# An output projection by seven products of half blocks in a transformer block kernel on one Trainium2 core

## The chip, the cores and the metric

The kernel runs on one core of a Trainium2 chip. The metric is device time in microseconds of one execution. Before the change three runs took 2075.6, 2077.8 and 2077.84 us; the median is 2077.8 us. The engines are named as the profile names them: PE (matrix products and transposes), PEld (its weight loads), DVE (vector engine), ACT (scalar engine), POOL and SP (the engine that issues nearly all DMAs here).

## The reference

One block on x of 512 positions by 2048 features, all in float32. What is computed:

```python
h = rmsnorm(x, g_attn)
proj = h @ w_in                                  # 2048 -> 6*1024 + 8
o_sb  = stick_breaking_attention(qa, ka, va)     # 8 heads of 128
o_fox = forgetting_attention(qf, kf, vf, log_f)  # 8 heads, softmax with a running bias
mixed = concat(head_rmsnorm(o_sb), head_rmsnorm(o_fox))    # 512 x 2048
x = x + mixed @ w_out                            # 2048 x 2048: the output projection
u = relu(rmsnorm(x, g_mlp) @ w_up)               # 2048 -> 8192
x = x + (u*u) @ w_down                           # 8192 -> 2048
return rmsnorm(x, g_final)
```

## The kernel before

Each float32 operand is split into a high part, a cast by ACT into a format that PE multiplies quickly (L63), and a low part, source minus high part by DVE (L64). A product is then three matmuls: high by high, high by low, low by high (`mm3`, L95 to L98). So each block of weights costs one DMA, one ACT cast, one DVE subtraction and its matmuls.

The stages on PE, in order: the projections of queries, keys and values, with the 16 attention heads laid between them (to about 627 us); the output projection (627 to 816 us); the up projection in 32 units (816 to 1400 us); the down projection (to 2010 us); the tail.

The output projection (`out_product`, L230) is plain. For each of four column blocks of 512 it loads 8 pieces of w_out (two rows of 128 by 512 columns), splits them and the matching two heads of `mixed`, and multiplies: 4 row blocks of 128 positions by 16 heads by 3 matmuls, into four banks `acco`. After a column block the residual is added (`x2`, L587), the sum is transposed back (`tr`, L597), and `a_form` makes the seven left sides that the up projection needs, split into `fh` and `fl`.

The up projection already multiplies by a scheme of seven products (Strassen and Winograd): a unit takes a 2 by 2 arrangement of blocks of w_up and needs sums of them. For 24 of the 32 units (`early`, L156) these sums are made during the projections: `drip` (L159) loads three blocks into the buffer `mix` (`sums`), does three DVE subtractions (L173 to L175) and stores the result in DRAM (`td`). The other 8 units load the blocks as they are ("raw" units) and do the three subtractions in the up stage (L677, L678, L680). `Unit.product` is one product: 8 matmuls of 512 columns with the high weights (against high and low left sides side by side) and 8 of 256 columns with the low ones.

The order of PE's instructions is written out for the projections and heads: `in_turn` yields after each piece with its nominal time, and parts of heads are put in when their step's time has come (`tc.manual_schedule`, L540). All else (DVE, ACT, SP, and PE in the later stages) is ordered by the compiler's scheduler; each engine executes its list in order, and each SP list entry is issued in order. A tile pool gives memory back when its `__exit__` runs; a tile that takes its place must wait for the last reader (`mixp_cm.__exit__`, L613, then `rw`, L620).

The forgetting heads need a bias row on all partitions: `bias_of` (L351) makes it by a matmul with a selector (`ck`) and an ACT copy (`cb`).

Of the kernel before, what the change touches and what calls it, by code (L numbers as in the profile page):

```python
# [14 lines left out]
P = 128  # L15
# [4 lines left out]
NH = 8  # L20
# [11 lines left out]


# [5 lines left out]
def block_kernel(ctx, tc, x, g_attn, w_in, b_f, g_out_sb, g_out_fox, w_out, g_mlp, w_up, w_down, g_final, y):  # L39
# [105 lines left out]
    md = [dp.tile([P, NT], F32, name=f"md{h}") for h in range(2 * NH)]  # L145
    td = [dp.tile([P, 3, KC // 2, P], F32, name=f"td{u}") for u in range(NU)]
    up_rows = w_up.rearrange("(a i p) f -> i p a f", i=2, p=P)

    def load_sums(u, i):

        r = mixp.tile([P, 3, KC // 2, P], F32, tag=f"x{i % 2}", name="sums")
        for j, (i, c) in enumerate(((0, 2 * u), (0, 2 * u + 1), (1, 2 * u + 1))):
            sp.dma_start(r[:, j], up_rows[i][:, :, c * P:(c + 1) * P])
        return r

    early = [u for u in range(NU) if u % 4 != 3]  # L156
    drops, raws, waiting = [0], {}, []

    def drip(low, load):  # L159

        drops[0] += 1
        i, j = divmod(drops[0] * 4 - 20, 9)
        with tc.issue_after(load.ins):
            if drops[0] == 2:
                raws.update((k, load_sums(early[k], k)) for k in range(2))
            if waiting and (waiting[0][0] <= drops[0] or (j < 4 and waiting[0][1] == i)):
                k = waiting.pop(0)[1]
                raws[k] = load_sums(early[k], k)
        if j > 3 or not 0 <= i < len(early):
            return  # L170
        b11, b12, b22 = (raws[i][:, j] for j in range(3))
# [4 lines left out]
        sp.dma_start(td[early[i]], raws.pop(i))  # L176
        if i + 2 < len(early):
            waiting.append((drops[0] + 2, i + 2))

    with (  # L180
        tc.tile_pool(name="hp", bufs=1) as hp,
        tc.tile_pool(name="att", bufs=1, side="right") as at,
    ):
# [14 lines left out]
        def accumulate_v(c0, m, steps, prepare=None, more=None):  # L198
# [7 lines left out]
            for j, step in enumerate(steps):  # L206
                k0, k1 = k1, k1 + step
                if prepare is not None:
                    prepare(k0, step)
                w = load_w([w_in[k0 * P:(k0 + step) * P, c:c + m // len(c0)].rearrange("(a p) c -> p a c", p=P) for c in c0],  # L210
                           step, m)
                held += [(k0 + i, w[i]) for i in range(step)]
# [17 lines left out]
        def out_product(n, mixed):  # L230
            ps = [acc.tile([P, NT], F32, tag="acc", name="acco") for _ in range(TB)]
            held = []
            for k0 in range(0, 2 * NH, 2):
                e0 = order[k0]
                w = load_w(w_out[e0 * P:(e0 + 2) * P, n * NT:(n + 1) * NT].rearrange("(a p) c -> p a c", p=P), 2, NT)
                ms = []
                for i in range(2):
                    ms.append(u_tile((k0 + i) % 4))
                    split(*ms[i], mixed[k0 // NH][:, (k0 + i) % NH, :])
                held += [(k0 + i, ms[i], w[i]) for i in range(2)]  # L240
                if n == 0 and k0 == 0:
                    continue
                for t in range(TB):
                    ts = slice(t * P, (t + 1) * P)
                    for k, m, wk in held:
                        mm3(ps[t], m[0][:, ts], m[1][:, ts], *wk, k == 0, k == 2 * NH - 1)
                    yield len(held) * 3 * 0.2267
                held = []
            return ps
# [101 lines left out]
        def bias_of(h):  # L351
            ck = atp.tile([P, NT], F32, tag="o", name="ck")
            pe.matmul(ck, nsel[:, h, :], ckT, start=True, stop=True)
            cb = at.tile([P, NT], F32, tag="ul5", name="cb")
            act.copy(cb, ck)
            return cb

        def attend_fox(h, hc, here):
# [3 lines left out]
            for i, r in enumerate(rows(s)):  # L362
                dve.scalar_tensor_tensor(rows(w)[i], r, cq[:, i, h:h + 1], cb[:, :(i + 1) * P], op0=ALU.add, op1=ALU.add)
# [15 lines left out]
        order = [NH + h for h in (6, 7, 0, 1, 2, 3, 4, 5)] + list(range(NH))  # L379
# [4 lines left out]
        with tc.tile_pool(name="tr0", bufs=2, space=PSUM) as trp:  # L384
# [56 lines left out]
            nsel = at.tile([P, NH, P], F32R, name="nsel")  # L441
            sel = wide("w")[:, :NH * P].rearrange("p (a b) -> p a b", a=NH)
            pool.memset(sel, 0.0)
            for shift in (0, NH):
                pool.affine_select(out=sel, in_=sel, compare_op=ALU.not_equal, fill=-1.0, base=-shift,
                                   pattern=[[-1, NH], [0, P]], channel_multiplier=1)
            dve.tensor_copy(nsel, sel)

        with tc.tile_pool(name="attp", bufs=1, space=PSUM) as atp:
# [3 lines left out]
            chl = at.tile([P, TB, P], F32, name="chl")  # L453
            pool.memset(chl, 0.0)
            cr = at.tile([P, TB, NH], F32R, name="cr")
# [18 lines left out]
            act.copy(cr, cq)  # L474
            dve.tensor_copy(chl[:, :, :NH], cr.bitcast(F32))
            dve.tensor_tensor(chl[:, :, NH:2 * NH], cq, cr.bitcast(F32), op=ALU.subtract)
            ckT = at.tile([P, NT], F32R, name="ckT")

            def turn_bias():
                cT = atp.tile([P, NT], F32, tag="o", name="cT")  # L480
                for t in range(TB):
                    pe.transpose(cT[:, t * P:(t + 1) * P], chl[:, t, :], ident)
                act.copy(ckT, cT)

            U, CB = {}, {}
            late = {}
# [15 lines left out]
            def outputs():  # L502
                late["mixed"] = [mixp.tile([P, NH, NT], F32, tag=f"x{i}", name="mixed") for i in range(2)]
                for k in range(2 * NH - 2):
# [495 lines left out]
```

## Time and profile before

| | us |
|---|---|
| median of three runs | 2077.8 |
| the profiled execution, its own time | 2075.16 |
| its span, first to last instruction | 2073.1 |
| PE busy in it | 2053.1 |
| DVE busy | 1601.9 |
| ACT busy | 1071.9 |
| clock granted to PE, mean | 0.999 of full |

The busy time of PE comes from modelled ends of pipelined matmuls; the distance between the starts of two matmuls is the better price of one. Idle time of an engine matters only where PE waits for it.

### The profile page before, as it was taken

What the parts mean: (1) busy time and instruction counts of PE and PEld (TensorE: products, weight loads), DVE (VectorE), ACT (ScalarE), POOL (GpSimd) and SP (SyncE); (2) the same over time, 40 slices, a digit from 0 to 9 for tenths busy, and PEclk for the clock granted to TensorE, in tenths of its full rate; (3) what the DMA queues carried; (4) which work ended last, traced back from release to release, by engine and by line L of the source; (5) the groups of instructions that cost most, each with busy time, mean ns of one, the idle gap of its engine ahead of it and who ended that gap; (6) DMA issues with size and microseconds to landing.
All of it is one profiled execution on the core that took longest, in us unless ns stands there. A gap on an engine that the chain in (4) does not pass through costs nothing.

```text
span 2073.1 us, 26761 instructions
## 1 busy us (share of the span) xinstructions
PE 2053.1 (99%) x10292; PEld 1746.6 (84%) x10292; DVE 1601.9 (77%) x1827; ACT 1071.9 (52%) x1426; POOL 57.1 (3%) x77
## 2 busy tenths in 40 slices
PE   9999999999999999999999999999999999999998
PEld 8888888888888887888888888888888888888886
DVE  5747748748766657788888888888799989888885
ACT  6334434444546556666666666666744434443433
POOL 0000000001100000000000000000000000000003
PEclk9999999999999999999999999999999999999999
DMA  7948948948833445578778777778865764764732
GB/s 237 296 134 255 295 150 259 315 116 254 289 102 102 132 152 171 178 260 273 237 257 272 243 252 265 234 253 285 321 232 209 266 240 163 266 232 135 271 111 82
DMA packets 356575, 455.88 MB, mean 220 GB/s; under 512 B 11440, under 2 KB 255200, under 8 KB 347360
## 3 DMA queue, kind: packets, MB, share of 16 engines
q1 hardware_dynamic: 355488, 452.05, 65.9%
q10 hardware_dynamic: 960, 2.13, 0.3%
q8 instruction: 81, 1.33, 0.2%
q14 instruction: 46, 0.38, 0.0%
HBM read 347.17 MB, written 106.95 MB: 219 GB/s over the span
## 4 chain that ended last, share of the span: by engine, by line
PE 90%; DVE 4%; DMA 3%; issue 2%; ACT 1%; SPq 0%; ACTq 0%; DVEq 0%
PE psa L687 9%; PE accd L96 8%; PE accd L98 8%; PE accd L97 8%; PE accq L96 5%; PE accq L98 5%; PE accq L97 5%; PE psa L689 5%; PE psc L687 4%; PE acco L97 3%; PE acco L98 3%; PE acco L96 3%; PE accv L96 3%; PE accv L97 3%; PE accv L98 3%; PE psc L689 2%
## 5 line engine op out<-in xcount | busy, mean ns | idle before, releaser
L63 ACT CAST wh<-wraw 128x1024 fp32r<-128x1024 f32 (+2 forms) x133 | 135.4, 1018 | 196.1 <-PE accq L97 115.5
L63 ACT CAST wh<-wd 128x1024 fp32r<-128x1024 f32 (+1 forms) x136 | 135.1, 1000 | 182.8 <-PE accd L98 120.6
L64 DVE TENSOR_TENSOR wl<-wraw,wh 128x1024 fp32r<-128x1024 f32 (+2 forms) x133 | 157.9, 1188 | 81.2 <-ACT wh L63 78.7
L64 DVE TENSOR_TENSOR wl<-wu,wh 128x1024 fp32r<-128x1024 f32 x166 | 201.8, 1223 | 17.7 <-PE psa L689 5.4
L63 ACT CAST wh<-wu 128x1024 fp32r<-128x1024 f32 x166 | 172.1, 1049 | 72.6 <-PE psa L687 25.1
L96 PE MATMUL accq<-hH,wh 128*128 128x512 f32 x512 | 201.2, 393 | 0.0
L98 PE MATMUL accq<-hH,wl 128*128 128x512 f32 x512 | 200.1, 391 | 0.0
L97 PE MATMUL accq<-hL,wh 128*128 128x512 f32 x512 | 199.8, 390 | 0.0
L64 DVE TENSOR_TENSOR wl<-wd,wh 128x1024 fp32r<-128x1024 f32 (+1 forms) x136 | 155.8, 1156 | 39.2 <-ACT wh L63 38.9
L96 PE MATMUL accd<-wh,uf 128*128 128x512 f32 x436 | 169.8, 389 | 1.0 <-issue 1.0
L97 PE MATMUL accd<-wl,uf 128*128 128x512 f32 x436 | 169.7, 389 | 0.0
L98 PE MATMUL accd<-wh,uf 128*128 128x512 f32 x436 | 169.7, 389 | 0.0
L63 ACT CAST wx<-wd 128x1024 fp32r<-128x1024 f32 (+1 forms) x88 | 87.5, 1000 | 119.7 <-PE accd L98 77.6
L64 DVE TENSOR_TENSOR wx<-wd,wx 128x1024 fp32r<-128x1024 f32 (+1 forms) x88 | 101.1, 1156 | 22.8 <-ACT wx L63 22.7
L98 PEld LDWEIGHTS accq<-hH,wl 128*128 128x128 f32 x512 | 96.1, 188 | 20.1
L97 PEld LDWEIGHTS accq<-hL,wh 128*128 128x128 f32 x512 | 96.2, 188 | 19.2
L96 PEld LDWEIGHTS accq<-hH,wh 128*128 128x128 f32 x512 | 96.3, 188 | 18.9
L97 PE MATMUL accd<-wx,uf 128*128 128x512 f32 x284 | 110.5, 389 | 0.0
L98 PE MATMUL accd<-wx,uf 128*128 128x512 f32 x284 | 110.5, 389 | 0.0
L96 PE MATMUL accd<-wx,uf 128*128 128x512 f32 x284 | 110.4, 389 | 0.0
L788 DVE TENSOR_TENSOR m<-m,accd 128x1024 f32<-128x1024 f32 x84 | 102.4, 1219 | 10.2 <-PE accd L98 10.1
L687 PE MATMUL psa<-fl,wh 128*128 128x512 f32 x388 | 106.0, 391 | 1.1 <-DVE fl L64 1.1
(288 smaller groups left out, 4859.0 us busy)
## 6 DMA issues: line engine op xcount, KB each, us to landing
ufd<-st SPq DMA_DIRECT2D x98, 512.0 KB, 5.9
wd<-in_w_down_dram SPq DMA_DIRECT2D x48, 1024.0 KB, 5.9
wraw<-in_w_in_dram SPq DMA_DIRECT2D x84, 512.0 KB, 4.8
uf<-ufd SPq DMA_DIRECT2D x42, 1024.0 KB, 7.2
sums<-in_w_up_dram SPq DMA_DIRECT2D x72, 512.0 KB, 6.0
td<-sums SPq DMA_DIRECT2D x24, 1536.0 KB, 7.9
wu<-td SPq DMA_DIRECT2D x71, 512.0 KB, 5.1
wu<-in_w_up_dram SPq DMA_DIRECT2D x32, 1024.0 KB, 7.7
```

What stands on the lines that cost most here:

```text
L63: ins = casts[0] = act.copy(hi, src)
L64: lows[0] = dve.tensor_tensor(lo, src, hi.bitcast(F32), op=ALU.subtract)
L96: pe.matmul(out, sh, mh, start=first, stop=False, skip_group_check=True)
L97: pe.matmul(out, sh, ml, start=False, stop=False, skip_group_check=True)
L98: pe.matmul(out, sl, mh, start=False, stop=last, skip_group_check=True)
L687: pe.matmul(ps, hi[:, a, :], both, start=a == 0 and p in (1, 2, 5), stop=False, skip_group_check=True)
L689: pe.matmul(ps[:, :2 * P], lo[:, a, :], F[p][a // 4][:, a % 4, 0, :], start=False, stop=a == KC // 2 - 1, skip_group_check=True)
L788: dve.tensor_tensor(M[p][:, :, db, :], M[p][:, :, db, :], ps, op=ALU.add)
```

## The change

The output projection becomes seven products, too. The 16 heads are two halves of 8 in the inner dimension, the 512 positions two halves of 256, and w_out has two halves of rows and, in each half of its columns (c = 0, 1), two blocks of 512 columns. A product p for a half c is 4 pieces (j) of 12 matmuls: 2 row blocks of 128 by 2 heads by 3. The left sides are made by `left(p, j)` from `mixed`, the sums of the weights by `drip` during the projections (8 units "out" of four DVE subtractions, stored in `tw`, among the units "up"). `LEFT_AT`, two more pools and `first_raw` place the buffers. The raw units of the up stage are now 12 (u modulo 8 in 2, 5, 7). One unit is dripped every 3 pieces of projection weights, in the value projections too. The residual and the transposes go by half blocks (`turn_block`), and the left sides of the up projection are made by `up_form`. All of the output projection and the first products of units 0 and 1 are in PE's written order. The bias row `cb` is now loaded by a DMA from DRAM (`cd`) that copies it to all partitions.

```diff
-    early = [u for u in range(NU) if u % 4 != 3]
+    early = [u for u in range(NU) if u % 8 not in (2, 5, 7)]
+    while ups_left or outs_left:
+        units.append(("out", outs_left.pop(0)) if len(units) % 7 in (1, 4) else ("up", ups_left.pop(0)))
...
+            if kind == "out":
+                dve.tensor_tensor(r[:, 3], r[:, 3], b22, op=ALU.subtract)
+        sp.dma_start(td[at_] if kind == "up" else tw[at_[0]][at_[1]], r)
...
+        def out_product(ps, p, c, js, start, stop):
+            for j in js:
+                hi, lo = out_piece(p, c, j)
+                for t in range(2):
+                    ts = slice(t * P, (t + 1) * P)
+                    for i in range(2):
+                        k = 2 * j + i
+                        ah, al = (w[:, i, ts] for w in late[1, j]) if (1, j) in late and p == 1 else (w[:, k, ts] for w in LT[p])
+                        mm3(ps[t], ah, al, hi[:, i], lo[:, i], start and k == 0, stop and k == NH - 1)
+                yield 12 * 0.2267
...
-            ck = atp.tile([P, NT], F32, tag="o", name="ck")
-            pe.matmul(ck, nsel[:, h, :], ckT, start=True, stop=True)
-            cb = at.tile([P, NT], F32, tag="ul5", name="cb")
-            act.copy(cb, ck)
+            cb = at.tile([P, NT], F32, tag="cb", name="cb", bufs=2)
+            sp.dma_start(cb, cd[h:h + 1, :].to_broadcast([P, NT]))
...
+            def before_outputs():
+                late["mixed"] = [mixp.tile([P, NH, NT], F32, tag=f"x{i}", name="mixed") for i in range(2)]
+                for k in range(2 * NH - 4):
+                    load_mixed(k)
+                left(1, 0)
+                left(1, 1)
...
+                left(1, 2, 2)
+                late["A"] = [[acc.tile([P, NT], F32, tag="acc", name="acca") for _ in range(2)] for c in range(2)]
...
+                for c in range(2):
+                    for j in range(4):
+                        yield from out_product(late["A"][c], 1, c, [j], True, True)
+                        if c == 0 and j < 3:
+                            left(5, j)
+                            left(6, j)
+                    add(late[1, 1, c], late["A"][c])
...
+    for c in range(2):
+        for j in range(4):
+            run_all(out_product(A[c], 4, c, [j], False, True))
+            if (c, j) in ((0, 0), (0, 1)):
+                turn_block(1, 2 * j + 1, r22[j])
+                for p in (5, 6, 7, 4):
+                    up_form(p, 2 * j + 1)
...
+            if (c, j) == (1, 1):
+                turn_block(1, 0, r21[0])
+                for p in (5, 6, 7, 4):
+                    up_form(p, 0)
+        add(r21[c], A[c])
...
+    u0, u1 = Unit(0), Unit(1)
+    u0.product(1)
+    turn_block(1, 2, r21[1])
+    u0.product(2)
+    for p in (5, 6, 7, 4):
+        up_form(p, 2)
+    u1.product(1)
...
+    u1.product(2)
+    for n in (1, 3, 0, 2):
+        up_form(3, n)
+    mixp_cm.__exit__(None, None, None)
...
+    rw = ctx.enter_context(tc.tile_pool(name="rw", bufs=5, side="right", reuse_waits="tile"))
...
+    u0.others()
+    u1.others()
+    for who, p in ((u0, 5), (u0, 6), (u0, 7), (u1, 5), (u0, 4), (u1, 6), (u0, 3), (u1, 7)):
+        who.product(p)
```

Three places of the instruction order. First, DVE at the end of the last value projection, where `vl` is the low part of the values of the last two heads (four of them, one for each 128 positions), `w` and L344 (L400 after the change) are the scans of a stick-breaking head, and `wl` is the low part of a piece of weights. Before:

```order
L67 SCALAR_TENSOR_TENSOR vl<-accv,r1v,vh 128x256
L344 SCALAR_TENSOR_TENSOR w<-w 128x256
L344 SCALAR_TENSOR_TENSOR w<-w 128x384
L344 SCALAR_TENSOR_TENSOR w<-w 128x512
L64 TENSOR_TENSOR wl<-wraw,wh 128x1024
L344 SCALAR_TENSOR_TENSOR w<-w 128x128
L67 SCALAR_TENSOR_TENSOR vl<-accv,r1v,vh 128x256
L345 TENSOR_TENSOR w<-s,w 128x1280
```

After, from the third `vl` to the fourth; `al` is the low part of a left side, and `r` holds the sums of heads that L283 makes:

```order
L400 SCALAR_TENSOR_TENSOR w<-w 128x128
L66 TENSOR_TENSOR al_5299<-mixed,ah_5298 128x1024
L66 TENSOR_TENSOR al_5323<-r,ah_5322 128x512 x2
L401 TENSOR_TENSOR w<-s,w 128x1280
L66 TENSOR_TENSOR wl<-wraw,wh 128x1024
L66 TENSOR_TENSOR al_5323<-r,ah_5322 128x512
L66 TENSOR_TENSOR al_5321<-mixed,ah_5320 128x1024
L283 TENSOR_TENSOR r<-r,mixed 128x512
L66 TENSOR_TENSOR al_5321<-mixed,ah_5320 128x512
L283 TENSOR_TENSOR r<-r,mixed 128x512
L69 SCALAR_TENSOR_TENSOR vl<-accv,r1v,vh 128x256
```

Between the last two `vl` stood four scans and one piece of weights; now splits and sums of the left sides and the subtraction of L401 stand there as well. On PE the product that reads the last `vl` follows 24 matmuls of 512 columns and 11 of its own after the last matmul of `accv`, before and after the change.

Second, SP at the passage from the output projection to the up units. `wq` and `wu` are blocks of w_up or of their sums `td`, `xd` the stores of the residual. Before:

```order
L86 DMA wraw<-in_w_out_dram 128x2x512 x2
L656 DMA wq<-in_w_up_dram 128x8x128
L664 DMA wq<-td_110 128x1024
L664 DMA wu<-td_110 128x1024 x2
L607 DMA xd_5676<-x_6458 128x2048
L646 DMA wu<-in_w_up_dram 128x8x256
L656 DMA wu<-in_w_up_dram 128x8x128
```

After, where the first `wu` takes memory that `mixed`, and then the up stage's input `h0` and `h1`, held:

```order
L811 DMA wq<-in_w_up_dram 128x8x128
L811 DMA wq<-td_111 128x1024
L811 DMA wq<-td_112 128x1024
L675 DMA xd_5697<-r 128x512 x2
L855 DMA wu<-td_111 128x1024 x2
L856 DMA wu<-in_w_up_dram 128x8x256
L855 DMA wu<-td_112 128x1024 x2
L856 DMA wu<-in_w_up_dram 128x8x256
L834 DMA wu<-in_w_up_dram 128x8x128
```

The first five loads of units 0 and 1 go to buffers `wq` of their own; the `wu` loads stand together behind them, and all later loads behind those.

Third, DVE at the same passage after the change: the last left sides of the up projection (`fl3`, from `h0`), and the weights that follow:

```order
L66 TENSOR_TENSOR fl5_6520<-s12_6903,fl5_6520 128x2x256
L66 TENSOR_TENSOR fl7_6266<-h1_6252,fl7_6266 128x2x256
L702 TENSOR_TENSOR s12_6903<-s12_6903,h0_6057 128x512
L897 TENSOR_TENSOR s1_6936<-s1_6936,psb_6839 128x512
L703 TENSOR_TENSOR h0_6057<-h0_6057,s12_6903 128x2x256
L891 TENSOR_TENSOR c_6880<-s1_6936 128x256
L66 TENSOR_TENSOR fl6_6264<-s12_6903,fl6_6264 128x2x256
L66 TENSOR_TENSOR fl3_6765<-h0_6057,fl3_6765 128x2x256
L66 TENSOR_TENSOR wl_7028<-wu_6994,wh_7027 128x1024
L66 TENSOR_TENSOR wl_7050<-wu_6994,wh_7049 128x1024
```

The last split from `h0` stands right ahead of the first weights from a `wu`; from the end of the seventh product of the output projection (p = 7) to that split DVE has 11 operations of 128x1024, 44 of 128x512 (or 128x2x256), 2 of 128x256 and three of four columns.

## Rows read from the trace of the kernel before

**Rows 1.** The page: busy time by engine, and the chain that ended last.
```profile
PE 2053.1 (99%) x10292; PEld 1746.6 (84%) x10292; DVE 1601.9 (77%) x1827; ACT 1071.9 (52%) x1426; POOL 57.1 (3%) x77
...
PE 90%; DVE 4%; DMA 3%; issue 2%; ACT 1%; SPq 0%; ACTq 0%; DVEq 0%
```
**Rows 2.** Windows by stage: length, busy PE, PEld, DVE, ACT, POOL, clock, DMA, GB/s.
```profile
400.00:559.00 159.00, 157.86 (x747) 131.76 (x746) 108.21 (x115) 72.73 (x85) 14.76 (x16) 1.00 0.72 230
559.00:640.00 81.00, 80.83 (x477) 71.57 (x476) 48.97 (x56) 43.18 (x53) 7.37 (x12) 1.00 0.31 92
640.00:700.00 60.00, 60.00 (x282) 50.12 (x282) 40.08 (x53) 38.43 (x62) 0.00 (x0) 1.00 0.42 132
816.00:900.00 84.00, 82.36 (x469) 71.61 (x468) 70.67 (x90) 55.36 (x76) 0.00 (x0) 1.00 0.71 233
1100.00:1400.00 300.00, 298.73 (x1711) 262.93 (x1711) 255.37 (x327) 196.02 (x252) 0.00 (x0) 1.00 0.76 251
```
**Rows 3.** Timeline of PE, 800 to 832 us: start, length, what, idle before.
```profile
799.75 0.39 PE L97 MATMUL acco<-wl,uh 128*128 128x512 f32 x1
...
814.26 0.40 PE L98 MATMUL acco<-wh,ul 128*128 128x512 f32 x1
814.49 1.91 PE L597 MATMUL tr<-ident,x 128*128 128x128 f32 x16
...
820.93 0.73 PE L687 MATMUL psa<-fl,wh 128*128 128x512 f32 x2 [1.06 <-DVE fl L64]
```
**Rows 4.** Groups by line and form: count, busy us, mean ns, idle before.
```profile
L63 ACT CAST wh<-wu 128x1024 fp32r<-128x1024 f32 x166 | 172.1, 1049 | 72.6 <-PE psa L687 25.1
...
L96 PE MATMUL acco<-wh,uh 128*128 128x512 f32 x256 | 98.7, 391 | 0.0
...
L64 DVE TENSOR_TENSOR ul<-mixed,uh 128x512 fp32r<-128x512 f32 x64 | 43.4, 689 | 30.7 <-PE acco L97 23.5 <-ACT uh L63 3.6 <-PE acco L98 3.6
...
L173 DVE TENSOR_TENSOR sums<-sums 128x1024 f32<-128x1024 f32 x24 | 29.7, 1236 | 2.0 <-DMA sums<-in_w_up_dram 2.0
```
**Rows 5.** Timeline of DVE, 626 to 642 us, around the last value splits.
```profile
630.35 0.48 DVE L67 SCALAR_TENSOR_TENSOR vl<-accv,r1v,vh 128x256 fp32r<-128x256 f32 x1
...
634.94 0.46 DVE L67 SCALAR_TENSOR_TENSOR vl<-accv,r1v,vh 128x256 fp32r<-128x256 f32 x1
635.31 1.48 DVE L345 TENSOR_TENSOR w<-s,w 128x1280 f32<-128x1280 f32 x1
```
**Rows 6.** Timeline of PE there: first `acco` after `accv`, and last of the head's product.
```profile
628.64 0.40 PE L96 MATMUL acco<-wh,uh 128*128 128x512 f32 x1
...
636.22 0.28 PE L98 MATMUL o<-ph,vl 128*128 128x128 f32 x1
```
**Rows 7.** Timeline of DVE, 816 to 832 us, at the passage to the up units.
```profile
818.46 1.22 DVE L64 TENSOR_TENSOR wl<-wu,wh 128x1024 fp32r<-128x1024 f32 x1
819.59 0.68 DVE L574 TENSOR_TENSOR hr<-hr 128x512 f32<-128x512 f32 x1
820.19 1.89 DVE L64 TENSOR_TENSOR fl<-hr,fl 128x512 fp32r<-128x512 f32 x3
```
**Rows 8.** DMA issues of the whole span: count, KB each, us to landing.
```profile
wu<-td SPq DMA_DIRECT2D x71, 512.0 KB, 5.1
wu<-in_w_up_dram SPq DMA_DIRECT2D x32, 1024.0 KB, 7.7
```
**Rows 9.** The same, of 815 to 830 us alone, with its mean rate.
```profile
DMA packets 3346, 4.93 MB, mean 329 GB/s; under 512 B 96, under 2 KB 2831, under 8 KB 3215
...
wu<-td SPq DMA_DIRECT2D x4, 512.0 KB, 7.1
```
**Rows 10.** Windows at the end of the span, columns as in rows 2.
```profile
2060.00:2065.00 5.00, 4.04 (x18) 3.00 (x16) 3.46 (x4) 0.95 (x4) 2.73 (x2) 1.00 0.51 210
2065.00:2070.00 5.00, 0.00 (x0) 0.00 (x0) 2.16 (x7) 2.32 (x6) 0.00 (x0) 0.91 0.23 88
2070.00:2073.00 3.00, 0.00 (x0) 0.00 (x0) 0.00 (x0) 0.00 (x0) 0.00 (x0) 0.50 0.53 204
```

More of the change, by code (lines that the diff above doesn't have):

```diff
@@ L228, in all_of @@
                     return e.value
[L230 to L243, printed above, removed]
-                    ts = slice(t * P, (t + 1) * P)
[L245 to L249, printed above, removed]
+        spares, raw_turn = [], [0]
@@ new lines, in left_tile, with left @@
+        def left_tile(p, pool_):
+            LT[p] = tuple(pool_.tile([P, NH, 2 * P], F32R, tag=f"f{q}{LEFT_AT[p]}", name=f"a{q}{p}") for q in "hl")
+        def left(p, j, k=1):
+            m0, m1 = late["mixed"]
+            ks = slice(2 * j, 2 * (j + k))
+            a11, a21, a12, a22 = (m[:, ks, i:i + 2 * P] for m in (m0, m1) for i in (0, 2 * P))
+            s = late["s"][j] if p in (5, 6, 3) else None
+            if p == 5:
+                dve.tensor_tensor(s, a21, a22, op=ALU.add)
+            if p == 6:
+                dve.tensor_tensor(s, s, a11, op=ALU.subtract)
+            if p == 7:
+                dve.tensor_tensor(a21, a11, a21, op=ALU.subtract)
+            if p == 3:
+                dve.tensor_tensor(a12, a12, s, op=ALU.subtract)
+            if p == 1 and j < 2:
+                out = [at.tile([P, 2, 2 * P], F32R, tag=f"a{q}{j}", name=f"a{q}1") for q in "hl"]
+                late[1, j] = out
+            else:
+                out = [LT[p][q][:, ks] for q in range(2)]
+            split(*out, {1: a11, 2: a12, 5: s, 6: s, 3: a12, 7: a21, 4: a22}[p])
@@ L378, in block_kernel @@
         o0 = 3 * WSB
-        order = [NH + h for h in (6, 7, 0, 1, 2, 3, 4, 5)] + list(range(NH))
+        late = {}
         def v_columns(h):
@@ L500, in values, with residual @@
                     V.update(zip(pairs, take_v(ps, len(pairs))))
[L502 to L506 removed]
+            def residual(h, n, tiles):
+                for t in range(2):
+                    sp.dma_start(tiles[t], xq[:, 2 * h + t, n * NT:(n + 1) * NT])
+                return tiles
@@ L508, in in_turn, with add @@
+            def add(r, ps):
+                for t in range(2):
+                    dve.tensor_tensor(r[t], r[t], ps[t], op=ALU.add)
             def in_turn():
@@ new lines, in block_kernel, with run_all @@
+    pc_cm = tc.tile_pool(name="pc", bufs=4, space=PSUM, reuse_waits="tile")
+    pc = pc_cm.__enter__()
+    A = late["A"]
+    spares[:] = [lambda q=q: hx.tile([P, 2, NT], F32, tag=f"hx{q}", name="wraw") for q in range(2)]
+    def run_all(steps):
+        for _ in steps:
+            pass
+    out_cm = tc.manual_schedule(engines={pe.engine})
+    out_cm.__enter__()
+    left(2, 3)
+    left(5, 3)
+    left(6, 3)
+    C = [[pc.tile([P, NT], F32, tag="pc", name="accc") for _ in range(2)] for c in range(2)]
@@ new lines, in block_kernel @@
+    left_tile(3, form_b)
+    r11 = [late[1, 1, c] for c in range(2)]
+    for c in range(2):
+        for j in range(4):
+            run_all(out_product(C[c], 2, c, [j], True, True))
+            left(3, 2 * c + j // 2) if j % 2 else None
+        add(r11[c], C[c])
+    r22p = [sgs[0].tile([P, 2, 2, NT], F32, tag="c", name="r22")][0]
+    r22 = [residual(1, 2 * c + 1, [r22p[:, c, t] for t in range(2)]) for c in range(2)]
+    left_tile(7, FP[5])
+    C = [[pc.tile([P, NT], F32, tag="pc", name="accc") for _ in range(2)] for c in range(2)]
@@ new lines, in block_kernel @@
+    for c in range(2):
+        for j in range(4):
+            run_all(out_product(C[c], 5, c, [j], True, False))
+            if j % 2:
+                left(7, 2 * c + j // 2)
+        add(r22[c], C[c])
+    r12 = [residual(0, 2 * c + 1, two(c)) for c in range(2)]
+    H[0] = mixp.tile([P, 4, 4, 2 * P], F32, tag="x0", name="h0")
+    for c in range(2):
+        run_all(out_product(C[c], 3, c, range(4), False, True))
+        add(r12[c], C[c])
+    left_tile(4, form_b)
+    for c in range(2):
+        run_all(out_product(A[c], 6, c, [3], False, False))
+        left(4, 2 * c, 2)
+        add(r12[c], A[c])
```

338 lines of the change are left out of this document (214 added, 124 removed).

## Prediction

> **What bounds the kernel now.** I began with the page: PE is busy for 99% of the span and makes 90% of the chain that ended last [rows 1]. The windows by stage show the same in every stage, at a full clock: in the 60 us from 640 us, inside the output projection, PE has no idle time, while DVE and ACT are busy for two thirds and the DMA share is 0.42 [rows 2]. So a matmul that goes is worth its whole price, as long as DVE, ACT and the loads still arrive in time. The one place of some length where PE loses time is the passage to the up units: 84 us from 816 us hold 82.4 us of PE, a loss of 1.6 us, where PE waits for left sides that DVE splits [rows 2, 3]. DVE is the engine to watch: there it is busy for 71 of 84 us, and for 255 of 300 us in the up stage [rows 2].
>
> **What goes from PE.** The output projection has 3 x 256 = 768 matmuls [rows 4]; 64 starts lie in the timeline between 799.75 and 814.26 us, so one costs 14.51 / 64 = 0.227 us [rows 3]. Seven products of 2 halves, 4 pieces and 12 matmuls are 672. The difference, 96, is 21.8 us. The eight `ck` matmuls of 512 columns are 1.8 us more. The transposes stay 64. Together PE has 23.6 us less to do, and nothing on PE is added.
>
> **What is added elsewhere.** In the projections, eight units "out" have 4 subtractions of 128x1024 each and there are four "up" units less with 3 each: 20 more on DVE, 1.24 us each [rows 4], 25 us over some 480 us in which DVE is busy for 0.68 (108 of 159 us) [rows 2]. Each unit now takes 3 pieces of 24 matmuls, 16.3 us; an "out" unit loads and stores 2 MB each way, 4.2 MB in 16.3 us or 257 GB/s, and the pieces of w_in add 0.52 MB in 5.4 us, 96 GB/s. That is 353 GB/s for the two "out" units in seven; before, an "up" unit of 3.1 MB in 2.25 pieces (12.2 us) asked for the same 353. PE did not suffer from it, and only the three buffers of projection weights are urgent. I put the projections at 0, and bound them at 0 to +5 us. The bias rows come by 256 KB DMAs of which the trace has no like; the 512 KB loads land in 5.1 us [rows 8], and a head's turn comes later than that. No gain, no loss, up to 1 us late. The split work of the output projection changes form (64 splits of `mixed` go; 24 splits of left sides, 16 sums of heads, 12 more residual sums and 24 more pieces of weights come) and is hidden while DVE keeps up with 2.72 us per piece. Adding up DVE's list against PE's by these durations, it keeps up from the second product on; it fails at two places.
>
> **First place: the last values.** Before, DVE ends the third `vl` at 630.83 us and the fourth at 635.40 us; PE's product with it reaches its last matmul at 636.22 us, 0.8 us later, or 7.6 us behind the end of `accv` at 628.64 us [rows 5, 6]. After the change these stand between the two splits as well: two of 128x1024 at 1.24 us, four of 128x512 and two sums at 0.69 us, and the subtraction of 1.48 us that used to come behind [rows 4, 5]: 2.48 + 4.14 + 1.48 = 8.1 us. The fourth `vl` would end at about 643.5 us on the clock of before, and PE needs it at 636.2. All work of PE behind that product waits, since its order is written. The wait is 7.3 us by full durations; where DVE runs without gaps its operations start closer, 0.60 us for 128x512 and 1.13 us for 128x1024 [rows 7], which makes 6.4. I take 7.0.
>
> **Second place: the passage to the up units.** Most left sides of the up projection are made while the output projection's last product (p = 4) and the first four products of units 0 and 1 run. From the end of the product before (p = 7) to the last split from `h0` DVE has 11 operations of 128x1024 and 44 of 128x512, some small ones beside: 11 x 1.24 + 44 x 0.69 + 1.3 = 45.3 us, or 41.2 us at the closer starts [rows 4, 7]; waits for PE's pieces and the transposes in its first part add about 2 us to the latter. I take 44.5 us. PE's list up to unit 0's product 6 is 96 x 0.227 = 21.8 us, four groups of 8 transposes at 0.12 us (1.91 / 16) are 3.8 less some overlap, say 3.4 [rows 3], and five products of 8 matmuls of 512 and 8 of 256 columns are 2.77 each with 0.12 for the short one: 39 us. The weights of product 6 are the first `wu`, which takes the memory of `h0` and so can only be issued after that last split. Its 512 KB land 5.1 us after issue over the whole run, and 7.1 us in the crowd of 815 to 830 us [rows 8, 9]; I take 6.0. Then the cast of 1.05 us [rows 4], in all 44.5 + 6.0 + 1.1 = 51.6 us against 39: PE stands for 12.6 us (41.2 + 2 + 5.1 + 1.1 makes 10.4; 46 + 7.1 + 1.1 makes 15.2). A first part of it shows at product 5 as a wait for `fl5`. The 1.6 us of before go, so the net is +11.0.
>
> **The clock.** At the end of the run PE works until about 2064.0 us; the granted clock is 1.00 on average to 2065, 0.91 over the next 5 us and 0.50 after, so it fell from 2.4 to 1.2 GHz near 2069, some 5 us into the idle time [rows 10]. Both waits are longer. What follows would run at the lower level for a while; how long no row shows. One product at half speed costs 2.8 us more. I take +1 us for each, between 0 and 2.8. The Trainium skill's page "TensorE: Matmul & The Clock Gate" (HAM oscillation — how this bites in real kernels) has the rule that idle gaps of PE should be kept short, since work behind a long one starts cold; the trace agrees that idleness lowers the clock, and by that rule the same +1 to +3 us would stand at each wait.
>
> **The rest.** The raw units are 12 instead of 8, so 12 more subtractions, 15 us of DVE over 580 us in a stage where it is at 0.85 [rows 2]; some raw units have waited for their load by tenths of a us or by 1.3 us. I put +0.5 us, bounds 0 and +3.
>
> **Sum.** -23.6 + 7.0 + 11.0 + 2.0 + 0.5 = -3.1 us. The profiled execution took 2075.16 us itself, so 2072.1 us there; it was 2.6 us under the median of the runs, so against that 2077.8 - 3.1 = 2074.7. I forecast 2074 us. The bounds: -23.6 + 6.4 + 8.8 = -8.4 us (2069), and -23.6 + 7.3 + 13.6 + 5.6 + 3 = +5.9 us (2084).
>
> **Rivals.** (1) The waits are small: if DVE's list really runs as far ahead as it did before (in the 640 us window it had 20 of 60 us free [rows 2]), PE gets all of its 23.6 us: 2054 us; with only one of the two waits 2063 to 2067. For it speaks that PE waited nowhere for long; against it that both waits are counted from lists that the engines execute in order. (2) Slower, by the load queue at the passage: behind that first `wu` stand the other loads of units 0 and 1, then all of unit 2, which is raw: 6 transfers of 4.2 MB and 4 of 2.1 MB, 6.3 MB in all, before unit 2's product 5. PE has some 25 us of products in that time. At the 329 GB/s of rows 9 they take 19 us and fit; at the 255 or so that the stage moves on average they take 25 us, and three subtractions (3.7 us) follow, so PE waits again, 4 to 8 us, and the clock falls a third time. Together with the upper bounds above 2082 to 2090. It decides where the queue moves less than about 290 GB/s. (3) The projections don't hide their 21 MB more and 25 us of DVE: the heads' softmax comes late, +5 to +8 us on the sum, 2079 to 2083 us. For it speaks a DMA share of 0.72 before; against it PE's 157.9 of 159 us [rows 2].
>
> **How the numbers follow.** A run of this kernel can tell no less than about 0.2%, 4.2 us. The forecast, both waits, holds 0.56: its own range 2069 to 2084, of that 0.24 below 2073.6, 0.29 within 0.2% and 0.03 above. Rival 1 holds 0.22, all faster. Rival 2 holds 0.15, all slower but 0.02. Rival 3 holds 0.07, 0.03 within and 0.04 slower. The sums are 0.46 faster (0.24 + 0.22), 0.34 the same (0.29 + 0.02 + 0.03), 0.20 slower (0.03 + 0.13 + 0.04). The range of 8 in 10 leaves out the best of rival 1 and the worst of rival 2: 2058 to 2085.
>
> **What would show it.** In the profile after: a wait of PE of 6 to 8 us at the product of the 15th head (o, released by DVE `vl`), soon after the last `accv`. A wait of 10 to 15 us some 180 us later, in two parts, the first at `psc` released by DVE `fl`, the second at `psa` released by ACT's cast of a `wu` whose DMA was issued right after a DVE split from `h0`. A clock below 1.00 in the windows behind both. No wait of over 1.5 us in the projections, nor between. DVE's busy time in the passage near 0.95 of it. I am wrong if PE's idle time in the two places is under 3 us each, or if a wait of the same size stands elsewhere.

## The result, and the profile after

The changed kernel takes 2079.73 us (median of 16 runs, 2077.4 to 2082.78); the kernel before took 2075.36 us beside it (16 runs). The ratio is 1.0024, 95% interval 1.0017 to 1.0031: slower by 4.4 us, where 2074 us and a gain of 3.1 us were forecast (the 2074 us stand on the three runs of before with a median of 2077.8 us). The profiled execution took 2079.36 us, its span 2077.6 us.

The page of the changed kernel, busy time by engine (against [rows 1]):

```profile
PE 2037.3 (98%) x10188; PEld 1730.4 (83%) x10188; DVE 1656.2 (80%) x1866; ACT 1074.7 (52%) x1419; POOL 69.0 (3%) x73
```

PE has 104 instructions and 15.8 us of busy time less, DVE 54.3 us more. At 0.227 us each the 104 are the 23.6 us of the forecast; that busy time fell by less is in part due to matmuls that now run at the lower clock and count as longer. The span grew by 4.5 us. What PE waited for shows where the gain went (line waited for, total us, times, longest). The waits of before at the same two stages:

```profile
PE psb L687 <- ACT wh L63: 1.2, 1, 1.2
...
PE psa L687 <- DVE fl L64: 1.1, 1, 1.1
...
PE psa L687 <- ACT s L693: 0.2, 1, 0.2
```

After:

```profile
PE psa L878 <- ACT s L884: 7.1, 6, 1.8
PE psa L878 <- ACT wh L65: 6.7, 1, 6.7
PE o L100 <- DVE vl L69: 6.0, 1, 6.0
...
PE psc L878 <- DVE fl L66: 1.7, 1, 1.7
PE psc L878 <- ACT wh L65: 1.4, 1, 1.4
```

Three things are new. The wait for `vl` and the two waits at the passage (`fl`, then the cast of a `wu`) are those that the prediction named. The first row is not: six waits of PE for the copy of `psa`. One of them, 0.7 us, still belongs to the passage; the other five and the 1.4 us for a cast stand in the up stage.

**The first place.** Timeline of PE around the product of the 15th head (start, length, what, idle before):

```profile
634.96 0.27 PE L99 MATMUL o<-pl,vh 128*128 128x128 f32 x1
641.22 0.47 PE L100 MATMUL o<-ph,vl 128*128 128x128 f32 x1 [5.99 <-DVE vl L69]
641.49 0.73 PE L98 MATMUL acca<-wh,ah 128*128 128x512 f32 x1
642.03 0.63 PE L99 MATMUL acca<-wl,ah 128*128 128x512 f32 x1
642.45 0.63 PE L100 MATMUL acca<-wh,al 128*128 128x512 f32 x1
...
646.23 0.39 PE L100 MATMUL acca<-wh,al 128*128 128x512 f32 x1
646.46 0.39 PE L98 MATMUL acca<-wh,ah 128*128 128x512 f32 x1
```

and DVE there:

```profile
632.30 1.19 DVE L66 TENSOR_TENSOR al<-mixed,ah 128x1024 fp32r<-128x1024 f32 x1
...
639.49 0.68 DVE L66 TENSOR_TENSOR al<-mixed,ah 128x512 fp32r<-128x512 f32 x1
640.10 0.68 DVE L283 TENSOR_TENSOR r<-r,mixed 128x512 f32<-128x512 f32 x1
640.70 0.47 DVE L69 SCALAR_TENSOR_TENSOR vl<-accv,r1v,vh 128x256 fp32r<-128x256 f32 x1
```

The value split stands behind 8.4 us that DVE does without a gap (splits, sums, the subtraction of L401 and one piece of weights), and PE behind it. The four scans that stood between the last two value splits before still do, from 629.3 to 632.3 us; the list of the change shows only the last of them. After the wait matmuls of 512 columns start 0.43 us apart, not 0.227 us [rows 3], until 646.2 us. The windows show the granted clock (columns as in [rows 2]):

```profile
637.00:639.00 2.00, 0.00 (x0) 0.00 (x0) 2.00 (x4) 0.46 (x1) 1.47 (x1) 1.00 0.39 41
639.00:640.00 1.00, 0.00 (x0) 0.00 (x0) 1.00 (x2) 0.40 (x1) 1.00 (x1) 0.66 0.90 346
641.00:643.00 2.00, 1.78 (x5) 1.49 (x6) 2.00 (x3) 1.64 (x3) 2.00 (x2) 0.50 0.00 0
646.00:647.00 1.00, 1.00 (x6) 0.84 (x5) 1.00 (x3) 0.34 (x1) 1.00 (x1) 0.92 1.03 381
```

PE's last matmul ended at 635.2 us. A mean of 0.66 from 639 to 640 us puts the fall from 2.4 to 1.2 GHz at 639.3 us, about 4 us into the idle time, and it stayed low for some 5 us of work: eleven matmuls took 4.7 us (641.49 to 646.23) instead of 2.5, so the clock cost 2.2 us.

**The second place.** The chain that ended last runs through it as forecast (start, us, what):

```profile
818.80 1.21 DVE fl L66 x2
820.01 0.02 issue
820.03 3.75 DMA wu<-td
...
823.80 1.05 ACT wh L65
...
824.90 3.78 PE psa L878 x8
```

The last split from `h0` ends at 820.0 us, the load is issued at once, lands in 3.75 us (6.0 were assumed; from 810 to 820 us the DMA engines had moved next to nothing), and the eight matmuls behind take 3.78 us instead of 1.84, again at the lower clock:

```profile
819.00:821.00 2.00, 0.00 (x0) 0.00 (x0) 1.00 (x2) 0.12 (x1) 0.00 (x0) 0.81 0.04 6
821.00:822.00 1.00, 0.00 (x0) 0.00 (x0) 0.00 (x0) 0.00 (x0) 0.00 (x0) 0.50 0.84 143
```

PE had ended its last matmul at 818.25 us, after a wait of 1.7 us shortly before. So here the clock fell about 2 us into the idle time, not 4.

**The up stage.** Windows 860 to 1400 us, first of the kernel before:

```profile
860.00:1400.00 540.00, 538.57 (x3084) 474.06 (x3084) 459.24 (x585) 352.59 (x453) 0.00 (x0) 1.00 0.76 252
```

then of the changed kernel:

```profile
860.00:1400.00 540.00, 532.13 (x3045) 467.59 (x3044) 465.39 (x585) 347.50 (x450) 0.00 (x0) 1.00 0.76 249
```

PE stands for 7.9 us here, 1.4 before, though DVE's busy share hardly differs. The waits are of two kinds. In the first, ACT waits for the last sum of a raw unit; the waits of 1.7 us at 1011.7 and at 1332.1 us are of it, and one of 0.3 us at 1170.2 us stands close behind such a sum. The one at 1011.7 us, first ACT:

```profile
1005.61 2.00 ACT L65 CAST wh<-wu 128x1024 fp32r<-128x1024 f32 x2 [3.64 <-DVE wu L871]
...
1011.12 0.56 ACT L884 COPY s<-psa 128x512 f32<-128x512 f32 x1
```

then DVE and PE:

```profile
1002.48 1.89 DVE L66 TENSOR_TENSOR st<-c,st 128x512 fp32r<-128x512 f32 x3
1004.28 1.22 DVE L871 TENSOR_TENSOR wu<-wu 128x1024 f32<-128x1024 f32 x1
```

```profile
1011.74 1.20 PE L878 MATMUL psa<-fh,wx 128*128 128x512 f32 x4 [1.67 <-ACT s L884]
```

The unit's first subtraction (L868, 997.3 us) had waited 0.9 us for its load; from there DVE had no gap, so the last one (L871) came late. ACT's cast of that sum stood 3.6 us at the head of its list, all else on ACT moved back, and PE waited for the copy that frees `psa`. Neither engine is full on average: the wait is made by the order of two lists.

The second kind is the waits at 1091.2, 1205.3 and 1252.0 us, 4.2 of the 7.9 us. No subtraction of a raw unit ran in the 30 us before any of them, and DVE itself was idle for 2.5 to 3.6 us just ahead. There ACT waits (4.1, 6.6 and 2.2 us) for a store of a hidden left side, whose buffer `st` it needs. The last of the three, in the chain, on ACT and on PE:

```profile
1239.61 8.29 DMA ufd<-st
```

```profile
1247.98 0.62 ACT L65 CAST st<-c 128x512 fp32r<-128x512 f32 x1 [2.22 <-DMA ufd<-st]
```

```profile
1251.97 1.20 PE L878 MATMUL psa<-fh,wx 128*128 128x512 f32 x4 [1.79 <-ACT s L884]
```

This store was issued right behind two 512 KB loads of a raw unit and took 8.3 us; the median of these stores is 5.3. So the raw units' own loads are a second candidate beside their subtractions.

The balance of the two profiled executions, from the distance of matmul starts beyond their undisturbed pitch: -23.6 us of work, +8.5 at the first place, +9.6 at the passage, +7.0 in the up stage (865 to 1400 us), +2.9 in all other stretches together; +4.4, and the spans differ by 4.5. These shares are an estimate, good to about half a us each.

### The profile page after: what moved, and what is told of

The parts are those of the page before. It is cut to its first block, busy times and chain, and to the rows that moved or that the text cites. A ratio compares the mean times of both kernels' runs of the same rounds, so it can differ in the third digit from the quotient of the medians.

```text
span 2077.6 us, 26773 instructions
## 1 busy us (share of the span) xinstructions
PE 2037.3 (98%) x10188; PEld 1730.4 (83%) x10188; DVE 1656.2 (80%) x1866; ACT 1074.7 (52%) x1419; POOL 69.0 (3%) x73
## 4 chain that ended last, share of the span: by engine, by line
PE 90%; DVE 4%; DMA 3%; ACT 2%; issue 1%; SPq 0%; ACTq 0%; DVEq 0%
PE psa L878 11%; PE accd L99 8%; PE accd L98 8%; PE accd L100 8%; PE psa L880 5%; PE psc L878 5%; PE accq L98 5%; PE accq L100 5%; PE accq L99 5%; PE psc L880 3%; PE psb L878 3%; PE accv L98 2%; PE accv L99 2%; PE accv L100 2%; PE psb L880 1%; PE m L99 1%
## 5 line engine op out<-in xcount | busy, mean ns | idle before, releaser
L65 ACT CAST wh<-wraw 128x1024 fp32r<-128x1024 f32 (+2 forms) x157 | 160.8, 1026 | 244.6 <-PE accq L99 118.5
L66 DVE TENSOR_TENSOR wl<-wraw,wh 128x1024 fp32r<-128x1024 f32 (+2 forms) x157 | 186.6, 1190 | 106.0 <-ACT wh L65 105.7
L98 PE MATMUL accd<-wh,uf 128*128 128x512 f32 x428 | 166.5, 389 | 0.7 <-issue 0.6
L100 PE MATMUL accd<-wh,uf 128*128 128x512 f32 x428 | 166.5, 389 | 0.0
L878 PE MATMUL psa<-fh,wh 128*128 128x512 f32 x392 | 107.9, 397 | 7.3 <-ACT wh L65 6.7
L99 PE MATMUL accd<-wx,uf 128*128 128x512 f32 x292 | 113.9, 390 | 0.5 <-DVE wx L66 0.3
L98 PE MATMUL accd<-wx,uf 128*128 128x512 f32 x292 | 113.6, 389 | 0.2 <-ACT wx L65 0.2
L100 PE MATMUL accd<-wx,uf 128*128 128x512 f32 x292 | 113.6, 389 | 0.0
```

The lines of the kernel that those rows point to most:

```text
L65: ins = casts[0] = act.copy(hi, src)
L66: lows[0] = dve.tensor_tensor(lo, src, hi.bitcast(F32), op=ALU.subtract)
L98: pe.matmul(out, sh, mh, start=first, stop=False, skip_group_check=True)
L99: pe.matmul(out, sh, ml, start=False, stop=False, skip_group_check=True)
L100: pe.matmul(out, sl, mh, start=False, stop=last, skip_group_check=True)
L878: pe.matmul(ps, hi[:, a, :], both, start=a == 0 and p in (1, 2, 5), stop=False, skip_group_check=True)
```

## The experiments

All were timed in 5 rounds beside the kernel before, whose median was 2075.3, 2074.7, 2075.4 and 2074.6 us in the four groups; so times are also compared with the changed kernel's 2079.7 us.

**Values first.** The splits of the left sides are held behind the last value split (in `take_v`), and then behind the weights next to which the code writes them.

```diff
+            def behind(*a):
+                with tc.issue_after(casts[0].ins), tc.issue_after(lows[0].ins):
+                    left(*a)
...
-                left(1, 2, 2)
+                behind(1, 2, 2)
...
-                            left(5, j)
-                            left(6, j)
+                            behind(5, j)
+                            behind(6, j)
...
```

> The splits and sums of the output projection's left sides are held, on ACT and DVE, behind the last value split and then behind the weights of the piece they are written next to. Theory A, only the order makes the wait: the wait of 6.0 us at the product o of the 15th head falls under 1.5 us, the clock stays at 1.00 there, and the time falls by 6 to 8.5 us against the changed kernel. Rival B, DVE has too much to do in that stretch altogether, so the wait turns up again at a weights split some us later: the time falls by less than 3 us.

Measured 2089.0 us (ratio to before 1.007, 1.0057 to 1.0082), 9 us slower than the changed kernel. The wait for `vl` is gone, and PE stands further on, at the product of the 16th head:

```profile
PE o L99 <- ACT ph L65: 7.2, 1, 7.2
```

From 629.5 to 665 us DVE has no gap; the norm of the 15th head (L384 to L387) now stands among the left sides and ends at 660.7, and the cast of `ph` waits for it. The wait turned up again, as rival B has it, though at a cast and not at a weights split, and a loss of 9 us is more than either theory allowed. Whether any order would do is left open here; the last run below answers it.

**Buffers of their own.** Products 6 and 7 of units 0 and 1 get loads that need not wait for `h0`.

```diff
-            r = rw.tile([P, 2, KC // 2, P], F32, tag="rw", name="wu")
-            t1 = first_raw(td[u][:, 0])
-            for i, j in ((0, 2), (1, 1)):
-                sp.dma_start(r[:, i], td[u][:, j])
+            t1, t2, t3 = (first_raw(td[u][:, j]) for j in (0, 2, 1))
...
+            return lambda: sp.dma_start(raw, last)
...
-    for who, p in ((u0, 5), (u0, 6), (u0, 7), (u1, 5), (u0, 4), (u1, 6), (u0, 3), (u1, 7)):
+    for who, p in ((u0, 5), (u0, 6), (u0, 7), (u1, 5), (u1, 6), (u1, 7), (u0, 4), (u0, 3)):
```

> The sums for products 6 and 7 of units 0 and 1 are loaded into buffers that do not overlap h0 and h1, and unit 1's products 6 and 7 run ahead of unit 0's products 4 and 3, whose 1 MB load still waits for the last split. Theory A, the wait is the load that can only be issued after the last split from h0: the wait of 6.7 us for the cast of wu goes, as does the low clock behind it, and up to 3 us of waits for fl5 and fl6 stay; the time falls by 7 to 9 us. Rival B, the wait moves to the 1 MB load, which still is issued late: the time falls by less than 4 us.

Measured 2075.7 us (1.0004, 0.9995 to 1.0012), 4.0 us below the changed kernel. The 6.7 us for the cast of `wu` are gone and the clock stays at 1.00 from 810 to 840 us. What is left there is DVE's own lateness:

```profile
PE psa L875 <- DVE fl L66: 2.5, 1, 2.5
PE psc L875 <- DVE fl L66: 1.7, 1, 1.7
```

Of the passage's 12.3 us beyond the pitch 6.8 stay: the load and the clock made 5.5 us, the list of 55 large operations the rest. (The two profiled executions differ by 5.4 us, the medians by 4.0.) No wait for the 1 MB load came up. The mechanism of theory A is shown, with less than the forecast gain.

**No raw sums.** This kernel leaves out the 36 subtractions of the raw units; they read the stored sums of the unit before, and so no blocks of w_up for these sums.

```diff
+    for u in range(NU):
+        if u % 8 in (2, 5, 7):
+            td[u] = td[u - 1]
...
-            self.raw = u not in early
+            self.raw = False
```

> The 12 raw units read the sums of the unit before them in place of their own, with as many bytes, so their 36 subtractions on DVE are left out. Theory A, the waits of the up stage come from these subtractions: the six waits for the copy of psa (7.1 us) go, PE's idle time from 860 to 1400 us falls from 7.9 to under 2 us, and the time falls by 6 to 8 us. Rival B, they come from the stores of the hidden left sides or the loads: over 5 us of them stay.

Measured 2069.1 us (0.9972, 0.9961 to 0.9983): 10.6 us below the changed kernel. PE does not stand at all from 860 to 1400 us:

```profile
860.00:1400.00 540.00, 540.00 (x3098) 475.49 (x3097) 441.96 (x569) 354.49 (x458) 0.00 (x0) 1.00 0.77 255
```

So the raw units make all the waits of the up stage. That it is their subtractions alone, as theory A has it, is not shown. The bytes are as many as before, but the edit changed the loads as well: from 860 to 1400 us, 27 loads of 512 KB come from w_up in place of 58, and the DMA packets fall from 121911 to 97516. Subtractions and raw loads went together, and no run here parts them.

**Raw units all odd.**

```diff
-    early = [u for u in range(NU) if u % 8 not in (2, 5, 7)]
+    early = [u for u in range(NU) if u % 8 not in (3, 5, 7)]
```

> Still 12 raw units, but u modulo 8 in 3, 5, 7 instead of 2, 5, 7, so that all are the second of their pair and none falls into the unit in which the hidden left sides of the pair before are split and stored. Theory A, the place of a raw unit counts: the waits in units 10, 18 and 26 go, and the time falls by 2 to 4 us. Rival B, only the number of raw units counts: the time stays within 1.5 us.

Measured 2074.3 us (0.9996, 0.9986 to 1.0006), 5.4 us below the changed kernel, but over twelve runs from 2070.5 to 2080.6. The profiled one, at 2078.6 us, still has 7.3 us of waits for the copy of `psa` in seven pieces, though from 860 to 1400 us PE stands for 4.6 us instead of 7.9. That the place counts is likely by the times; how stays open.

**The kernel before with 12 raw units.**

```diff
-    early = [u for u in range(NU) if u % 4 != 3]
+    early = [u for u in range(NU) if u % 8 not in (2, 5, 7)]
```

> The kernel before with one edit: raw units are those with u modulo 8 in 2, 5, 7 (12 of them) as after the change, in place of the 8 with u modulo 4 equal 3. Nothing of the output projection is changed. Theory A, the raw units alone cost what the up stage lost: PE's waits in the up stage go from about 2 us to 7 to 10, the time rises by 5 to 8 us against the kernel before. Rival B, it takes the new passage or the new buffers as well: the time rises by less than 2 us.

Measured 2089.2 us (1.007, 1.0057 to 1.0082): 14.5 us more than the kernel before, with no change to the output projection. Theory A, and more than it said; PE stands for 12.2 us from 860 to 1400 us, and for 1.4 in the kernel before:

```profile
PE psa L687 <- ACT s L693: 10.2, 6, 3.8
...
PE psc L687 <- ACT wh L63: 2.8, 1, 2.8
```

**Raw sums on POOL.**

```diff
-            dve.tensor_tensor(self.b[7], self.b[7], self.b[5], op=ALU.subtract)
-            dve.tensor_tensor(self.b[5], self.b[5], self.b[1], op=ALU.subtract)
+            pool.tensor_tensor(self.b[7], self.b[7], self.b[5], op=ALU.subtract)
+            pool.tensor_tensor(self.b[5], self.b[5], self.b[1], op=ALU.subtract)
...
-            dve.tensor_tensor(self.b[6], self.b[6], self.b[5], op=ALU.subtract)
+            pool.tensor_tensor(self.b[6], self.b[6], self.b[5], op=ALU.subtract)
```

> The changed kernel with the 36 subtractions of the raw units on POOL, which is nearly idle, in place of DVE. Theory A, DVE's list is too full in raw units: the waits for the copy of psa go as in the run without these subtractions, and the time falls by 6 to 10 us. Rival B, the sums are late whoever makes them, or POOL takes much longer than DVE's 1.22 us for one: the waits stay or grow, and the time stays or rises.

Measured 2101.1 us (1.0125, 1.0111 to 1.0139), 21 us slower than the changed kernel. Groups by line and form:

```profile
L871 POOL TENSOR_TENSOR wu<-wu 128x1024 f32<-128x1024 f32 x12 | 37.3, 3110 | 0.9
...
L868 POOL TENSOR_TENSOR wu<-wu 128x1024 f32<-128x1024 f32 x12 | 32.1, 2672 | 691.6 <-DMA wu<-in_w_up_dram 550.5 <-DMA ufd<-st 105.3 <-DVE c L901 35.7
```

One takes 2.7 to 3.1 us, DVE's take 1.22; PE's waits for the copy of `psa` grow to 17.5 us. Rival B, the sums came later still. A test of a relieved DVE this is not: from 860 to 1400 us its busy time is 458.3 us against 465.4, in part since its other operations took longer beside a busy POOL (see the last section).

**Later sums.** As the first run, with the left sides of products 5 and 6 made in the second half of product 1.

```diff
-                        if c == 0 and j < 3:
-                            left(5, j)
-                            left(6, j)
+                        if c == 1 and j > 0:
+                            behind(5, j - 1)
+                            behind(6, j - 1)
```

> As the run that put the values first, but the left sides of products 5 and 6 are made during the second half of product 1 and not the first, so that less of DVE's work falls among the last heads. Theory A, DVE's work is too much only at that spot: neither the wait for vl (6.0 us) nor the wait for ph of the last head (7.2 us in the first try) is over 2 us, and the time falls by 5 to 8 us against the changed kernel. Rival B, the stretch from the last values to product 6 is full whatever the order: waits of over 4 us stay somewhere in it, and the time falls by less than 4 us.

Measured 2084.1 us (1.0048, 1.0034 to 1.0062), 5 us better than the first try and 4.3 us above the changed kernel. The wait for `vl` is gone; two shorter ones, 5.2 us together, stand later in the stretch, nearer to rival B than to theory A, and the time is above the changed kernel's, which neither forecast:

```profile
PE o L100 <- DVE pl L66: 3.2, 1, 3.2
...
PE acca L99 <- ACT ah L65: 2.0, 1, 2.0
```

**The same with these sums on POOL** (the four sums in `left` from `dve.` to `pool.`).

> As the run before it, with the sums of heads for the left sides (L281 to L287 of the changed kernel, 28 operations of 128x512 at most) on POOL in place of DVE. Theory A, DVE's load in that stretch is the limit: the waits fall further than without, to under 1.5 us in all, and the time falls by 7 to 9 us against the changed kernel. Rival B, POOL is slower than DVE and its sums arrive late: PE waits for a left side, and the time is 2 us or more above that of the run before it.

Measured 2088.7 us (1.0066, 1.0054 to 1.0079), 4.6 us above the run without POOL. A sum of 128x512 takes POOL 1.45 to 1.61 us, and PE waits for left sides (2.1 us) and longer at the passage. Rival B again.

**Eight raw units.** The changed kernel with the raw units of before, and a unit of sums every 2.6 pieces.

```diff
-    early = [u for u in range(NU) if u % 8 not in (2, 5, 7)]
+    early = [u for u in range(NU) if u % 4 != 3]
...
-        i, j = divmod(drops[0] - 6, 3)
-        if j or not 0 <= i < len(units):
+        i, j = divmod(drops[0] * 5 - 30, 13)
+        if j >= 5 or not 0 <= i < len(units):
```

> The changed kernel with the 8 raw units of the kernel before (u modulo 4 equal 3); the sums of the four more units are made in the projections, a unit every 2.6 pieces in place of every 3, so that all 32 fit. Theory A, the number of raw units costs what the up stage lost: its waits fall to about 2 us and the time falls by 7 to 10 us against the changed kernel. Rival B, the projections can't hide four more units (13 MB and 12 subtractions): PE waits in them by several us, and the time falls by less than 3 us.

Measured 2074.7 us (0.9995, 0.9986 to 1.0004), 5.0 us below the changed kernel. The up stage's loss is gone, and over half of it now stands in the projections, 6.1 us where the changed kernel lost 1.4:

```profile
400.00:627.00 227.00, 220.87 (x1113) 187.89 (x1112) 166.44 (x179) 104.85 (x124) 19.55 (x24) 0.99 0.80 266
860.00:1400.00 540.00, 540.00 (x3095) 475.25 (x3094) 459.73 (x587) 351.62 (x455) 0.00 (x0) 1.00 0.77 255
```

Both theories have a part: the fewer raw units give 8 us, and the four more units among the last heads take back some 5.

**Eight raw units and own buffers.**

> The run before together with the buffers of their own for products 6 and 7 of units 0 and 1. If the two causes add, the time falls by 10 to 14 us against the changed kernel, to 2066 to 2070 us, 0.3% and more under the kernel before; the wait for vl of 6.0 us stays. If they don't add (the up stage's waits take the place of the passage's), it stays within 3 us of the run before.

Measured 2069.4 us (0.9968, 0.9957 to 0.9979), 10.3 us below the changed kernel: 5.0 and 4.0 us add. This beats both kernels. What it still waits for:

```profile
PE o L100 <- DVE vl L69: 5.8, 1, 5.8
PE s L98 <- DVE pl L66: 5.7, 4, 2.8
```

**Sums made sooner**: a unit every 2.4 pieces (12 for 13 in the diff of the eight raw units).

> The run with 8 raw units and own buffers, with a unit of sums every 2.4 pieces in place of 2.6, so that the last units are done some 35 us sooner and the subtractions leave the last heads alone. Theory A, the 5.7 us of waits for pl between 525 and 625 us in that run come from the subtractions standing among the last heads' work on DVE: they fall under 2 us and the time falls by 3 to 5 us against that run (2069.4). Rival B, the loads can't come that fast (3.4 MB a unit in 13.1 us and 96 GB/s of weights are some 355 GB/s) and DVE waits for them in its list: the time stays or rises.

Measured 2070.4 us (0.9977, 0.9968 to 0.9986), no gain over 2069.4. The waits of scores for `pl` went from 5.7 to under 0.3 us and the loads kept up, as theory A has it; but the new order of DVE's list at the passage made the wait for `fl` 4.7 instead of 1.7 us and one for `psa` 3.3 us. What was won was given back at another place.

**One left side moved.** The eight raw units and own buffers, with only the splits for product 2 held back.

```diff
-                        if c == 0 and j == 0:
-                            left(2, 0, 2)
-                        if c == 0 and j == 1:
-                            left(2, 2)
+                        if c == 0 and j < 2:
+                            with tc.issue_after(casts[0].ins), tc.issue_after(lows[0].ins):
+                                left(2, 2 * j, 2 - j)
```

> The run with 8 raw units and own buffers, with the splits of the left side of product 2 alone (al2, two operations) held behind the weights of product 6, where the code writes them, instead of standing ahead of the last vl. Theory A, each operation taken from ahead of vl shortens PE's wait there by its length as long as its new place has room: the wait for vl falls from 5.8 to about 3 us (two sums move with them), and the time falls by 2 to 4 us. Rival B, DVE is full up to product 6, so the wait turns up at pl of the last head: the time changes by less than 1.5 us.

Measured 2065.8 us (0.996, 0.9946 to 0.9973), 3.6 us better and the best of all: 14 us below the changed kernel, 9 us below the kernel before. The wait for `vl` is shorter by what was moved, and none came up at the last head:

```profile
PE psc L874 <- DVE fl L66: 4.7, 1, 4.7
PE s L98 <- DVE pl L66: 4.0, 3, 2.2
...
PE o L100 <- DVE vl L69: 3.0, 1, 3.0
```

Theory A holds for this one move: order does count, and the first tries moved too much, into places that were full.

## Why the prediction was wrong

**What goes from PE** (-23.6 us) held: matmul counts and pitch are as worked out.

**The first place** (+7.0): a wait of 6.0 us, found at the named product and by the named release; the lower bound by the closer starts was the better price, since DVE ran without a gap. With the clock it came to 8.5, against 8.0 forecast.

**The passage** (+11.0 net, and +1 for the clock): place, order and release were as forecast, the size was not. The waits were 1.7 + 6.7 = 8.4 us, not 12.6, and under the lower bound of 10.4. DVE's list took 43.3 us (from about 776.7 to 820.0) where 44.5 were assumed, the load 3.75 where 6.0 were, and PE's own list 39.8 where 39 were. (The forecast's 41.2 us for DVE at the closer starts is a slip: 11 x 1.13 + 44 x 0.60 + 1.3 is 40.1.) With the clock and a short wait behind, PE lost 12.3 us beyond the pitch against 2.7 before, so 9.6 against 12.0 forecast.

**The clock** (+1 for each): it fell at both, and cost 2.2 us at the first and some 2.5 at the second, within the bounds.

**The step that failed** is the one called "The rest": 12 more subtractions "over 580 us in a stage where it is at 0.85", with "+0.5 us, bounds 0 and +3". Without the subtractions of all 12 raw units (and with other loads) the time is 10.6 us less, and PE's idle time in the up stage goes from 7.9 us to nothing; with 8 raw units it goes as well. The kernel before lost 1.4 us there and rose by 14.5 us with the same 12 units alone. So the four units more cost the up stage 6.5 us of PE's time, over twice the upper bound. The error was to price them by DVE's mean share over the stage, and by the waits of eight units that the order before had room for. In 3.3 of the 7.9 us, and likely 0.4 more, the three subtractions fall into a list that was full for some us already; ACT's cast waits at the head of its list for the last of them, and the copy that PE needs stands behind it. In the other 4.2 us a late store holds ACT, and whether the raw units' loads or their subtractions make it late stays open.

The sum missed by 7.5 us (+4.4 for -3.1): 6.5 by this term, 2.9 in stretches put at nothing, 0.5 at the first place, and 2.4 the other way at the passage. That the measured time lies within 2069 to 2084 us is the width of the range, not the forecast's merit: it is on the wrong side of no change. By its own sign ("a wait of the same size stands elsewhere") the forecast was wrong: the up stage's waits, though in six pieces of at most 1.8 us, add up to 7.9 us, more than the first place's 6.0. The rivals named three other mechanisms, none of them this one.

**The rivals.** Small waits (1): no. The queue of loads at the passage (2): no, PE does not wait between 831 us and the up stage's first wait at 1011.7 us, so unit 2's products were not late; the slower time has another cause. The projections (3): PE stood for 1.4 us in 227 us from 400 us on, as before, so at 28 units they hid their share; at 32 units in the same time they did not (the run with eight raw units).

## What to carry to other kernels

Work that is added to an engine with a mean share of 0.85 is not priced by the mean: look at the unit in which it falls, what its list holds in the 5 us before, which other engine has an instruction waiting for its result at the head of its own list, and which loads come with it. When a planned order moves a load or a split, look for the first instruction that needs a buffer of the stage before: that one, and the time at which its last reader runs, set the length of the passage. And a gain in matmuls is best tried with each of the other edits undone alone: here the seven products did give their 23.6 us, and the edit that made room for them cost 6.5 by the profile.

## What the runs showed of the hardware

POOL took 2.7 to 3.1 us for a float32 subtraction of 128x1024 for which DVE takes 1.22 us. In the 540 us in which POOL was busy with them for 84, DVE's splits of `wu` of the same size took 1.34 us on average where they had taken 1.22. The granted clock fell from 1.00 to 0.50 about 4 us into PE's idle time at the first place, and about 2 us into it at the second, where a wait of 1.7 us had come shortly before; both times it stayed at 1.2 GHz for some 5 us of dense matmuls behind the wait. A load of 512 KB for which the DMA engines stood idle landed in 3.75 us, and the two 1 MB loads behind it in 10.4 (median).
